# Later rows of a partition added to PSUM by VectorE in place of identity matmuls, with the pipeline drained at each tile

## Chip, cores, metric

One core of one Trainium2 chip. The metric is the device time of one execution in microseconds (us), the median of several runs. The kernel before takes 1262.9 us. Its runs agree within 0.1%.

## The reference

A running log-sum-exp along the second axis of a float32 array of shape (4, 4096, 4128). It equals the log of a running sum of exps:

```python
out[:, 0, :] = x[:, 0, :]
for t in range(1, S):
    mx = np.maximum(out[:, t - 1, :], x[:, t, :])
    out[:, t, :] = mx + np.log(np.exp(out[:, t - 1, :] - mx) + np.exp(x[:, t, :] - mx))
```

## The kernel before

A tile is 128 partitions by R rows by 4128 columns. R is 3 in 40 tiles and 2 in 4 tiles; the first tile and the last are two-row tiles. Partition p holds R consecutive rows. There are four tile buffers, so loads run three tiles ahead. A tile is worked on in four chunks of 1024 columns; the last chunk also has a tail of 32 columns. For each chunk ScalarE (ACT in the profile) takes the exp of all rows. TensorE (PE; its weight loads are PEld) then forms, in one of three PSUM buffers (`pt`, the memory that matmuls add into; `qt` is the same for the tail), the sum of everything up to the first row of each partition: triangular matmuls (`incl`, `excl`) over the rows, and a `pick` matmul for the carry. This group is called a head below.

The rows then come out one at a time, each in a "stage": ACT writes the Ln of the PSUM buffer to the tile, and then the next row's exps are added to the same buffer. In the kernel before, an identity matmul does that addition. After the last row VectorE (DVE) saves the last 32 partitions as the carry of the next tile, as a pair of fp16 values: a cast and a subtract.

```python
def keep(cr, pt):
    nc.vector.tensor_copy(cr[HI:HI + 32, :], pt[HI:HI + 32])
    nc.vector.tensor_tensor(out=cr[LO:LO + 32, :], in0=pt[HI:HI + 32],
                            in1=cr[HI:HI + 32, :], op=mybir.AluOpType.subtract)
# ... class Chunk
def stage(self, j):
    t, c, pt = self.t, self.c, self.pt
    nc.scalar.activation(t.xt[:, j, c * CH:(c + 1) * CH], pt, ACT.Ln)
    if j + 1 < t.r:
        for s in range(0, CH, MM):
            mm(pt[:, s:s + MM], ident, self.e(j + 1, s, s + MM), stop=j + 2 == t.r)
        if c == last and j == 0:
            nc.scalar.activation(t.xt[:, :, t0:D], self.qt, ACT.Ln)      # the tail Ln
            keep(carry_t, self.qt[:, t.r - 1, :])
    else:
        keep(carry[c], pt)
# ... the loop runs over the chunks of ALL tiles, three chunks in flight
for g in range(len(chunks) + R - 1):
    for d in range(R - 1, -1, -1):
        if 0 <= g - d < len(chunks) and d < chunks[g - d].t.r:
            k = chunks[g - d]
            k.stage(d)
            # ... after a tile's last stage: store it, load three tiles ahead
    if g + 2 < len(chunks):
        chunks[g + 2].exp()
    if g + 1 < len(chunks):
        chunks[g + 1].head()
```

The softmax here doesn't subtract the row's maximum and nothing guards it: scores larger than these inputs give would overflow.

## Time and profile before

| | before |
|---|---|
| time, median | 1262.9 us |
| queue's share of the 16 transfer engines | 99.4% |
| busy: ACT, PE, DVE | 947, 689, 451 us |
| one three-row tile: transfers, compute when not waiting | 29.2 us, 22.7 us |

The last row of the table is read from the exps of the last chunk. Their starts are 29.2 us apart on average in the steady state, and 22.7 us apart where two tiles run back to back.

The page of the kernel before follows. The line that begins with DMA is the mean busy share of the transfer engines in tenths, in 40 slices of the span (the time from the first to the last instruction). The two lines after the queue line are the chain that ended last, by engine and by instruction. The last two are groups: count, busy us, mean ns of one, idle time before them and its releaser.

```profile
span 1261.0 us, 6165 instructions
...
PE 688.7 (55%) x2268; PEld 237.0 (19%) x2268; DVE 451.4 (36%) x445; ACT 947.3 (75%) x733; POOL 2.2 (0%) x13
...
DMA  9999999999999999999999999999999999999998
...
q1 hardware_dynamic: 12672, 541.07, 99.4%
...
DMA 69%; ACT 21%; PE 5%; issue 2%; DVE 1%; SPq 0%; ACTq 0%
DMA xt<-in_x_dram 67%; ACT xt L128 11%; ACT xt L162 10%; PE pt L88 5%; DMA out_dram<-xt 2%; ACT xt L167 0%; SPq L116 0%; DVE carry L92 0%; DVE carry L93 0%; ACTq L231 0%; SPq L113 0%; ACTq L128 0%; PE qt L88 0%
...
L88 PE MATMUL pt<-xt,ident 128*128 128x512 f16 x672 | 251.3, 470 | 530.7 <-ACT xt L162 530.4
...
L93 DVE TENSOR_TENSOR carry<-pt,carry 32x1024 f16<-32x1024 f32 x176 | 215.9, 1227 | 6.1
```

The queue is full in every slice but the last, and loads are 67% of the chain: this kernel is held by its transfers. The skill's "DMA: Bandwidth & Descriptors", section "Where 436 GB/s comes from", gives 435 GB/s as the ceiling of the ports into SBUF. This trace moved 429 GB/s on average and 432 to 433 in a steady stretch, just under that figure, so it agrees.

From its waits view (engine, instruction, what it waited for, total us, times, longest):

```profile
ACT xt L128 <- DMA xt<-in_x_dram: 247.8, 42, 12.2
ACT xt L167 <- PE pt L88: 45.7, 44, 1.1
```

The first line is the slack: exps wait 248 us in total for loads, about 6 us per tile. The tail Ln (L167) reads only `qt`, yet in every tile it waits for a matmul on `pt`, the identity matmul issued just before it. (It writes the last 32 columns of `xt`; that matmul reads other columns of the same tile.)

### The profile page before, as it was taken

The page shows a single profiled execution, that of the slowest core. Times are in us where ns is not written, and L with a number is a line of the kernel's source. Part 1 is how long each engine was busy: PE and PEld are TensorE (multiplying, and loading weights), DVE is VectorE, ACT ScalarE, POOL GpSimd, SP SyncE. Part 2 cuts the span into 40 slices and gives each one's busy share as a digit, 9 for nine tenths or more (in the row PEclk, how much of TensorE's full clock was granted, in tenths as well). Part 3 has the DMA queues.
Part 4 walks back from the last instruction along what each step waited for, and adds up shares of the span by engine and source line. Part 5 has one row for each costly group of instructions (what it writes and reads, how often), then busy time and mean ns, then how long its engine had stood idle before and what let it go on. Part 6 is the DMA issues. An engine that isn't in the chain of part 4 may idle for free.

```text
span 1261.0 us, 6165 instructions
## 1 busy us (share of the span) xinstructions
PE 688.7 (55%) x2268; PEld 237.0 (19%) x2268; DVE 451.4 (36%) x445; ACT 947.3 (75%) x733; POOL 2.2 (0%) x13
## 2 busy tenths in 40 slices
PE   3665554555555555655346555555634755664552
PEld 1222111111121111211112211111211211221120
DVE  2443333333333333334424333333442433333344
ACT  5997777777777777778569777777966977777794
POOL 0000000000000000000000000000000000000000
PEclk9887777777677777777768777787777777778786
DMA  9999999999999999999999999999999999999998
GB/s 411 410 439 431 432 427 434 438 430 432 433 437 431 432 432 436 432 427 436 431 433 436 437 429 431 436 436 432 430 434 435 432 431 432 434 435 431 433 422 347
DMA packets 12702, 541.46 MB, mean 429 GB/s; under 512 B 1408, under 2 KB 1408, under 8 KB 1408
## 3 DMA queue, kind: packets, MB, share of 16 engines
q1 hardware_dynamic: 12672, 541.07, 99.4%
q8 instruction: 18, 0.29, 0.1%
q14 instruction: 12, 0.10, 0.0%
HBM read 270.53 MB, written 270.53 MB: 429 GB/s over the span
## 4 chain that ended last, share of the span: by engine, by line
DMA 69%; ACT 21%; PE 5%; issue 2%; DVE 1%; SPq 0%; ACTq 0%
DMA xt<-in_x_dram 67%; ACT xt L128 11%; ACT xt L162 10%; PE pt L88 5%; DMA out_dram<-xt 2%; ACT xt L167 0%; SPq L116 0%; DVE carry L92 0%; DVE carry L93 0%; ACTq L231 0%; SPq L113 0%; ACTq L128 0%; PE qt L88 0%
## 5 line engine op out<-in xcount | busy, mean ns | idle before, releaser
L128 ACT ACTIVATE xt<-xt 128x3072 f16<-128x3072 f32 (+3 forms) x176 | 478.5, 2719 | 247.9 <-DMA xt<-in_x_dram 247.8
L88 PE MATMUL pt<-xt,ident 128*128 128x512 f16 x672 | 251.3, 470 | 530.7 <-ACT xt L162 530.4
L162 ACT ACTIVATE xt<-pt 128x1024 f32<-128x1024 f32 x512 | 487.6, 1030 | 2.5 <-PE pt L88 0.7
L92 DVE CAST carry<-pt 32x1024 f16<-32x1024 f32 x176 | 216.4, 1230 | 761.0 <-ACT xt L162 760.7
L88 PE MATMUL pt<-xt,excl 128*128 128x512 f16 x672 | 247.0, 504 | 0.0
L93 DVE TENSOR_TENSOR carry<-pt,carry 32x1024 f16<-32x1024 f32 x176 | 215.9, 1227 | 6.1
L88 PEld LDWEIGHTS <-ident 128*128 128x128 f16 x672 | 70.1, 104 | 677.7 <-issue 654.0
L88 PE MATMUL pt<-xt,incl 128*128 128x512 f16 x352 | 152.0, 526 | 23.6 <-ACT xt L128 15.0
L88 PEld LDWEIGHTS <-excl 128*128 128x128 f16 x756 | 92.5, 124 | 141.0 <-issue 108.1
L88 PE MATMUL pt<-carry,pick 128*128 128x512 f16 x320 | 109.8, 429 | 0.0
L88 PEld LDWEIGHTS <-incl 128*128 128x128 f16 x480 | 45.2, 111 | 129.7 <-DVE carry L93 95.2
L88 PEld LDWEIGHTS <-pick 128*128 128x128 f16 x360 | 40.6, 113 | 57.0 <-issue 34.3
L167 ACT ACTIVATE xt<-qt 128x96 f32<-128x96 f32 (+1 forms) x44 | 10.9, 249 | 45.7 <-PE pt L88 45.7
L92 DVE CAST carry_t<-qt 32x32 f16<-32x32 f32 x44 | 8.7, 197 | 25.5 <-ACT xt L167 25.4
L88 PE MATMUL qt<-xt,incl 128*128 128x64 f16 (+2 forms) x128 | 12.3, 196 | 0.0
L88 PE MATMUL qt<-xt,excl 128*128 128x64 f16 (+1 forms) x84 | 10.6, 187 | 0.0
L93 DVE TENSOR_TENSOR carry_t<-qt,carry_t 32x32 f16<-32x32 f32 x44 | 8.5, 193 | 1.5
L88 PE MATMUL qt<-carry_t,pick 128*128 128x96 f16 (+1 forms) x40 | 8.2, 204 | 0.0
L83 DVE MEMSET carry<- 128x512 uint32 x4 | 1.9, 485 | 1.1 <-PEq L220 1.0
L70 ACT ACT_TABLE_LOAD x1 | 1.3, 1283 | 0.8 <-PEq L220 0.8
L35 POOL TENSOR_SCALAR_AFFINE_SELECT pick<-pick 128x128 f16<-128x128 f16 x2 | 0.6, 294 | 0.1
L25 POOL TENSOR_SCALAR_AFFINE_SELECT incl<-incl 128x128 f16<-128x128 f16 x1 | 0.3, 294 | 0.0
(11 smaller groups left out, 1.9 us busy)
## 6 DMA issues: line engine op xcount, KB each, us to landing
xt<-in_x_dram SPq DMA_DIRECT2D x40, 6192.0 KB, 42.2
out_dram<-xt SPq DMA_DIRECT2D x40, 6192.0 KB, 28.1
xt<-in_x_dram SPq DMA_DIRECT2D x4, 4128.0 KB, 37.3
out_dram<-xt SPq DMA_DIRECT2D x4, 4128.0 KB, 23.0
```

Source lines behind the costliest of these rows:

```text
L25: nc.gpsimd.affine_select(out=t, in_=t, pattern=[[1, P]], compare_op=mybir.AluOpType.is_ge, fill=0.0, base=base, channel_multiplier=-1,)
L35: nc.gpsimd.affine_select(out=t, in_=t, pattern=[[step, P]], compare_op=mybir.AluOpType.not_equal, fill=1.0, base=base, channel_multiplier=1,)
L70: nc.scalar.preload_act_table_set("natural_log_exp_and_others")
L83: nc.vector.memset(t, 0.0)
L88: nc.tensor.matmul(pt, lhsT=w, rhs=rhs, start=start, stop=stop, skip_group_check=True)
L92: nc.vector.tensor_copy(cr[HI:HI + 32, :], pt[HI:HI + 32])
L93: nc.vector.tensor_tensor(out=cr[LO:LO + 32, :], in0=pt[HI:HI + 32], in1=cr[HI:HI + 32, :], op=mybir.AluOpType.subtract,)
L128: nc.scalar.activation(self.t.half[:, :, 2 * c0:2 * c0 + w], self.t.xt[:, :, c0:c0 + w], ACT.Exp,)
L162: nc.scalar.activation(t.xt[:, j, c * CH:(c + 1) * CH], pt, ACT.Ln)
L167: nc.scalar.activation(t.xt[:, :, t0:D], self.qt, ACT.Ln)
```

## The change

The intent is to take the identity matmuls off TensorE, which needs a weight load for each, and to give the additions to VectorE, which is idle 64% of the time. The loop is rewritten tile by tile: each tile's stages all end before the next tile's first exp is issued. The diff, cut to its core:

```diff
-                for s in range(0, CH, MM):
-                    mm(pt[:, s:s + MM], ident, self.e(j + 1, s, s + MM), stop=j + 2 == t.r)
+                nc.vector.tensor_tensor(
+                    out=pt, in0=pt, in1=self.e(j + 1, 0, CH), op=mybir.AluOpType.add,
+                )
 ...
-    for g in range(len(chunks) + R - 1):
-        for d in range(R - 1, -1, -1):
-            if 0 <= g - d < len(chunks) and d < chunks[g - d].t.r:
-                k = chunks[g - d]
-                k.stage(d)
 ...
+    for n, s in enumerate(steps):
+        chunks = [Chunk(s, c) for c in range(n_main)]
+        chunks[0].exp()
+        chunks[1].exp()
+        chunks[0].head()
+        for g in range(n_main + s.r - 1):
+            for d in range(s.r - 1, -1, -1):
+                if 0 <= g - d < n_main:
+                    chunks[g - d].stage(d)
+            if g + 2 < n_main:
+                chunks[g + 2].exp()
+            if g + 1 < n_main:
+                chunks[g + 1].head()
+        s.store()
+        if n + ahead < len(steps):
+            steps[n + ahead].load()
```

The identity matrix and its construction go too. Bytes moved and work on ACT are unchanged.

More of the change, by code (lines that the diff above doesn't have):

```diff
@@ L29, in tri, with ones_at @@
         return t
-    def ones_where_zero(bases, step, name):
+    def ones_at(rows, name):
         t = pool.tile([P, P], FP16, name=name)
         nc.gpsimd.memset(t, 0.0)
-        for base in bases:
+        for row in rows:
             nc.gpsimd.affine_select(
-                out=t, in_=t, pattern=[[step, P]], compare_op=mybir.AluOpType.not_equal,
-                fill=1.0, base=base, channel_multiplier=1,
+                out=t, in_=t, pattern=[[0, P]], compare_op=mybir.AluOpType.not_equal,
+                fill=1.0, base=-row, channel_multiplier=1,
             )
@@ L43, in _constants @@
         tri(-1, "excl"),
-        ones_where_zero([0], -1, "ident"),
-        ones_where_zero([-(HI + 31), -(LO + 31)], 0, "pick"),
+        ones_at([HI + 31, LO + 31], "pick"),
     )
@@ L71 @@
     consts = ctx.enter_context(tc.tile_pool(name="consts", bufs=1))
-    incl, excl, ident, pick = _constants(nc, consts)
+    incl, excl, pick = _constants(nc, consts)
     bufs = 4
@@ L85, with mm @@
     ctx.enter_context(tc.manual_schedule())
-    def mm(pt, w, rhs, start=False, stop=False):
-        nc.tensor.matmul(pt, lhsT=w, rhs=rhs, start=start, stop=stop, skip_group_check=True)
+    def mm(pt, w, rhs, start=False):
+        nc.tensor.matmul(pt, lhsT=w, rhs=rhs, start=start, stop=False, skip_group_check=True)
     def keep(cr, pt):
@@ L182 @@
         assert row == S
-    chunks = [Chunk(s, c) for s in steps for c in range(n_main)]
     ahead = bufs - 1
@@ L187 @@
         s.load()
-    stored = 0
-    chunks[0].exp()
-    chunks[1].exp()
-    chunks[0].head()
-    for g in range(len(chunks) + R - 1):
-        for d in range(R - 1, -1, -1):
-            if 0 <= g - d < len(chunks) and d < chunks[g - d].t.r:
-                k = chunks[g - d]
-                k.stage(d)
-                if k.c == last and d + 1 == k.t.r:
-                    k.t.store()
-                    if stored + ahead < len(steps):
-                        steps[stored + ahead].load()
-                    stored += 1
-        if g + 2 < len(chunks):
-            chunks[g + 2].exp()
-        if g + 1 < len(chunks):
-            chunks[g + 1].head()
+    for n, s in enumerate(steps):
[14 more added lines that the diff above has]
+            steps[n + ahead].load()
 _INS = ['x']
```

## The prediction

> **What bounds it now.** The DMA queues. The profile's queue table gives the one data queue 99.4% of the span on 16 engines, 541 MB at 429 GB/s, and the slice view shows 9 tenths in every slice. The Trainium skill, "DMA: Bandwidth & Descriptors", section "Where 436 GB/s comes from", puts the port ceiling at 435 GB/s; the trace agrees. A tile of three rows per partition (R=3) moves 12.4 MB, about 29 us; two tiles take 58.5 us in the chain of waits. Compute fits inside: ACT is busy 947 us (75%), about 22 us per tile, DVE 451 us, and the waits view has ACT waiting 248 us for loads, mostly once every two tiles. Slack: about 6 us per tile.
>
> **What the change does.** It removes 672 identity matmuls (470 ns, 251 us of PE), off the critical path, and adds 336 VectorE adds over 128x1024. Their cost: the carry subtract has the same operands (fp32 PSUM, fp16 SBUF, 1024 columns) and took 1.227 us. The Trainium skill, "VectorE: DVE Perf Modes", errata section, gives (N+151)/0.96 for an fp32 tensor_tensor, 1224 ns here; agrees. At 1.25 us each: +420 us of DVE, to about 870 us. The next tile's exps and first matmuls no longer stand among this tile's last Lns.
>
> **Critical path.** No engine exceeds 29 us per tile in sum (ACT 22, DVE 20), but the chain does. One R=3 tile laid out by hand in program order (exp 2.76 us, next start 2.66 later; Ln 1.03, every 0.93; cold matmul 0.43, so 8 take 3.5; carry pair 2.5; hand-offs about 0.05):
> - exp0, exp1, then ACT waits about 1 us for the first chunk's matmuls; Ln, exp2, two Lns, exp3, Ln: 15.7 us.
> - From there VectorE leads: carry0, add, add, carry1, add, add (to 25.7 us). The tail Ln has a wait on VectorE in the new build, so it waits for the last of these adds and stands ahead of chunk 2's last Ln: carry2 starts at about 27.0, last add ends at 30.7.
> - The last Ln ends at 31.8; the next exp0 starts at about 31.7.
> R=2 tiles, likewise: 23 us. DMA needs 29 us per R=3 tile, so compute becomes the bound.
> Total: 27.7 (first exp, as before) + 40 x 31.7 + 4 x 23.0 + about 13 (last 4.1 MB store and end) = 1401 us, 11% slower.
>
> **Prediction:** 1400 us, 8 in 10 between 1365 and 1440. Chances: faster by over 2% 0.01, within 2% 0.03, slower by over 2% 0.96.
>
> **What would show each step.** Queue share falls to about 0.90 and GB/s to about 387; ACT's wait for loads falls to under 40 us. In its place ACT waits for VectorE adds (about 5 to 7 us per tile) and for first-chunk matmuls (about 1 us). Adds: 336, mean 1.2 to 1.25 us; DVE busy 850 to 880 us; ACT busy unchanged at about 947 us. The chain that ended last: DVE near half, ACT near half, DMA under 6%. Exp0 starts every 31 to 32 us in R=3 tiles.
>
> **What would make it wrong.** An add whose output is in PSUM has no record in this trace; if it costs 1.1 us, the period falls by about 0.8 us (1370), if 1.4, it grows by 0.8 (1435). A faster TensorE clock at the tile's start saves at most 1 us per tile (1360). If the tile period came under 29 us, DMA would bind again and the time would be the same as before, nearly 3 us below my layout. Late loads (stores holding the fourth buffer) would add time.

## The result and the profile after

The changed kernel takes 1382.3 us, against 1262.9 us for the kernel before: a ratio of 1.0945, with a 95% interval of 1.0926 to 1.0964. A ratio here is the mean time of one kernel's runs over that of the other's in the same rounds, so it is not quite the ratio of the medians that are quoted.

The page of the changed kernel, the same lines. The last but one is the new add; the identity group is gone.

```profile
span 1380.2 us, 5327 instructions
...
PE 482.2 (35%) x1596; PEld 182.3 (13%) x1596; DVE 853.4 (62%) x781; ACT 974.1 (71%) x733; POOL 1.8 (0%) x11
...
DMA  9999999999999999998999999999899999999847
...
q1 hardware_dynamic: 12672, 541.07, 93.2%
...
DVE 42%; ACT 42%; PE 10%; issue 4%; DMA 1%; ACTq 0%
ACT xt L126 25%; DVE pt L162 18%; ACT xt L160 16%; DVE carry L90 12%; DVE carry L91 12%; PE pt L86 10%; DMA xt<-in_x_dram 1%; ACT xt L166 1%; ACTq L227 0%; ACTq L166 0%; ACTq L160 0%
...
L162 DVE TENSOR_TENSOR pt<-pt,xt 128x1024 f32<-128x1024 f32 x336 | 402.0, 1229 | 316.5 <-ACT xt L160 312.4
...
L91 DVE TENSOR_TENSOR carry<-pt,carry 32x1024 f16<-32x1024 f32 x176 | 215.9, 1227 | 6.1
```

Transfers fell from 69% to 1% of the chain, and ACT and DVE share it in equal parts. No compute engine is busy more than 71% of the span. The busiest resource is still the queue, at 93%; run e4 shows that it no longer sets the time.

From its waits view:

```profile
ACT xt L160 <- DVE pt L162: 211.9, 88, 2.9
...
ACT xt L166 <- DVE pt L162: 117.5, 44, 3.0
ACT xt L160 <- PE pt L86: 32.3, 40, 0.9
...
ACT xt L126 <- DMA xt<-in_x_dram: 11.1, 1, 11.1
```

Exps (L126) wait once for a load, the first. Lns (L160) and the tail Ln (L166) wait for adds 329 us in total, 7.5 us per tile, and 32 us for the head of a tile's first chunk.

The second part of one three-row tile, on the timeline (start, duration, engine, line, operation, tiles, shapes, count merged, and idle time before with its releaser). L90 and L91 are a carry pair. Where ACT shows three Lns merged, they are of three different chunks.

```profile
650.55 2.85 ACT L160 ACTIVATE xt<-pt 128x1024 f32<-128x1024 f32 x3
651.61 1.23 DVE L90 CAST carry<-pt 32x1024 f16<-32x1024 f32 x1 [2.34 <-ACT xt L160]
652.87 1.23 DVE L91 TENSOR_TENSOR carry<-pt,carry 32x1024 f16<-32x1024 f32 x1
654.13 2.36 DVE L162 TENSOR_TENSOR pt<-pt,xt 128x1024 f32<-128x1024 f32 x2
...
655.40 3.14 ACT L160 ACTIVATE xt<-pt 128x1024 f32<-128x1024 f32 x3 [1.99 <-DVE pt L162]
...
656.52 1.23 DVE L90 CAST carry<-pt 32x1024 f16<-32x1024 f32 x1
...
657.79 1.23 DVE L91 TENSOR_TENSOR carry<-pt,carry 32x1024 f16<-32x1024 f32 x1
659.05 2.37 DVE L162 TENSOR_TENSOR pt<-pt,xt 128x1024 f32<-128x1024 f32 x2
...
661.50 0.25 ACT L166 ACTIVATE xt<-qt 128x96 f32<-128x96 f32 x1 [2.97 <-DVE pt L162]
661.65 1.93 ACT L160 ACTIVATE xt<-pt 128x1024 f32<-128x1024 f32 x2
...
662.70 1.23 DVE L90 CAST carry<-pt 32x1024 f16<-32x1024 f32 x1 [0.49 <-ACT xt L160]
663.97 1.23 DVE L91 TENSOR_TENSOR carry<-pt,carry 32x1024 f16<-32x1024 f32 x1
665.22 1.23 DVE L162 TENSOR_TENSOR pt<-pt,xt 128x1024 f32<-128x1024 f32 x1
666.49 1.02 ACT L160 ACTIVATE xt<-pt 128x1024 f32<-128x1024 f32 x1 [2.90 <-DVE pt L162]
667.41 3.84 ACT L126 ACTIVATE xt<-xt 128x2048 f16<-128x2048 f32 x2
```

From 651.61 to 666.45 VectorE has only two gaps of any size, 0.38 and 0.49 us, before and after the small tail carry (not shown) at 661.79. It works through carry, two adds, carry, two adds, the small tail carry, carry, add. ACT follows it: it waits 2 to 3 us at a time for one more buffer to be ready. The next tile's exp starts only behind the last Ln, at 667.41. In the first half of the tile it is the other way round: ACT is nearly always busy and VectorE has only three adds and the carry left over from the tile before. So neither engine is full over a tile, but one of the two is full at nearly all times.

### The profile page after: what moved, and what is told of

It reads as the page before. It is cut to its first block, busy times and chain, and to the rows that moved or that the text cites. A ratio compares the mean times of both kernels' runs of the same rounds, so it can differ in the third digit from the quotient of the medians.

```text
span 1380.2 us, 5327 instructions
## 1 busy us (share of the span) xinstructions
PE 482.2 (35%) x1596; PEld 182.3 (13%) x1596; DVE 853.4 (62%) x781; ACT 974.1 (71%) x733; POOL 1.8 (0%) x11
## 4 chain that ended last, share of the span: by engine, by line
DVE 42%; ACT 42%; PE 10%; issue 4%; DMA 1%; ACTq 0%
ACT xt L126 25%; DVE pt L162 18%; ACT xt L160 16%; DVE carry L90 12%; DVE carry L91 12%; PE pt L86 10%; DMA xt<-in_x_dram 1%; ACT xt L166 1%; ACTq L227 0%; ACTq L166 0%; ACTq L160 0%
## 5 line engine op out<-in xcount | busy, mean ns | idle before, releaser
L160 ACT ACTIVATE xt<-pt 128x1024 f32<-128x1024 f32 x512 | 505.0, 1023 | 263.4 <-DVE pt L162 211.9
L162 DVE TENSOR_TENSOR pt<-pt,xt 128x1024 f32<-128x1024 f32 x336 | 402.0, 1229 | 316.5 <-ACT xt L160 312.4
L126 ACT ACTIVATE xt<-xt 128x3072 f16<-128x3072 f32 (+3 forms) x176 | 475.5, 2701 | 12.5 <-DMA xt<-in_x_dram 11.1
L90 DVE CAST carry<-pt 32x1024 f16<-32x1024 f32 x176 | 216.4, 1230 | 175.4 <-ACT xt L160 174.1
L86 PE MATMUL pt<-xt,excl 128*128 128x512 f16 x672 | 259.2, 524 | 0.0
L91 DVE TENSOR_TENSOR carry<-pt,carry 32x1024 f16<-32x1024 f32 x176 | 215.9, 1227 | 6.1
L86 PEld LDWEIGHTS <-incl 128*128 128x128 f16 x480 | 53.3, 117 | 965.0 <-issue 926.1
L86 PE MATMUL pt<-carry,pick 128*128 128x512 f16 x320 | 128.1, 491 | 0.0
L86 PEld LDWEIGHTS <-excl 128*128 128x128 f16 x756 | 95.7, 128 | 146.7 <-issue 117.6
L166 ACT ACTIVATE xt<-qt 128x96 f32<-128x96 f32 (+1 forms) x44 | 10.9, 249 | 117.5 <-DVE pt L162 117.5
L86 PEld LDWEIGHTS <-pick 128*128 128x128 f16 x360 | 43.9, 122 | 64.8 <-issue 47.3
L90 DVE CAST carry_t<-qt 32x32 f16<-32x32 f32 x44 | 8.6, 196 | 16.8 <-ACT xt L166 16.8
L86 PE MATMUL qt<-xt,incl 128*128 128x64 f16 (+2 forms) x128 | 15.9, 233 | 0.0
L91 DVE TENSOR_TENSOR carry_t<-qt,carry_t 32x32 f16<-32x32 f32 x44 | 8.5, 193 | 1.5
```

The lines of the kernel that those rows point to most:

```text
L86: nc.tensor.matmul(pt, lhsT=w, rhs=rhs, start=start, stop=False, skip_group_check=True)
L126: nc.scalar.activation(self.t.half[:, :, 2 * c0:2 * c0 + w], self.t.xt[:, :, c0:c0 + w], ACT.Exp,)
L162: nc.vector.tensor_tensor(out=pt, in0=pt, in1=self.e(j + 1, 0, CH), op=mybir.AluOpType.add,)
```

## The experiments

The theory: a three-row tile's time is the longer of its transfers (29.2 us) and its compute period. The change lengthens the compute period in two ways, by adds on VectorE and by draining, and only the two together push it past 29.2 us. Rivals: the adds alone do it; the drain alone does it; transfers that come late set part of the new period. Each run was timed beside runs of its own of the kernel before, and differences within 2% count as "same".

All kernels were correct except e4 to e7, which leave most of the output unwritten. Their outputs are wrong, which doesn't matter for the times.

### e1: the adds alone

The identity matmuls in `stage` become the VectorE add as in the diff above; the loop over all chunks stays as before.

> The adds on VectorE, but the loop of the kernel before, so that the next tile's first exps and matmuls stand among this tile's last Lns. Theory (neither part alone takes a tile past the 29 us that its transfers take; only both together do): about 1263 us, 1255 to 1275, with the queue still above 98% of the span; a tile laid out by hand takes 25 to 26 us of compute. Rival (the adds alone put VectorE on the critical path): 1300 us or more, with ACT waiting for adds over 150 us and the queue below 96%.

Measured: 1276.6 us, ratio 1.0107 (1.0092 to 1.0123); queue 98.8%. This is just above the range given, and slower than before by 13.7 us, but far from the rival's 1300 us. One mark of the rival was met: ACT waited 152 us for adds, where it had over 150; its other two, time and queue share, were not. Where are the 13.7 us? Mostly at the two ends, where there is no queue of ready transfers to hide compute behind. The fourth store, which the loads behind it wait for, goes out at 121.6 us in place of 115.7, and the fifth at 151.0 in place of 144.9: about 6 us. In between the lag grows slowly, to 10.7 us at the last load: from 150 to 1190 us the queue's share is 1.00 in both kernels, but it moves 431 GB/s in place of 433, and the exps of the last chunk start 29.33 us apart on average in place of 29.19. The cause of this lag is not known. The last 3.6 us come at the end. In windows of 10 us (the columns are the busy us of PE, PEld, DVE, ACT and POOL, then the granted TensorE clock, the queue's share, which in so short a window can pass 1, and GB/s), the kernel before has

```profile
1230.00:1240.00 10.00, 6.73 (x22) 2.31 (x22) 7.75 (x8) 9.29 (x9) 0.00 (x0) 0.83 0.63 269
1240.00:1250.00 10.00, 1.90 (x12) 0.72 (x10) 6.48 (x7) 3.13 (x4) 0.00 (x0) 0.71 1.03 444
```

and the adds-only kernel has

```profile
1230.00:1240.00 10.00, 5.30 (x20) 2.02 (x20) 8.29 (x9) 6.77 (x7) 0.00 (x0) 0.77 0.84 362
1240.00:1250.00 10.00, 4.04 (x10) 1.26 (x11) 8.68 (x8) 9.53 (x9) 0.00 (x0) 0.57 0.39 168
```

Its queue is 61% idle from 1240 to 1250, while the last tile is still computed: its last Ln ends near 1263, against 1244 before. The period theory stands, but 1263 us was too simple: slower compute shows at the ends even when the transfers bind in between.

### e2: the drain alone

The loop of the changed kernel, with the identity matmuls kept.

> Identity matmuls as before, but the loop of the changed kernel, which finishes every tile before the next one's first exp. Theory: about 1263 us, 1255 to 1275, since a tile laid out by hand takes 25 to 27 us of compute, under the 29 us of its transfers. Rival (draining is what costs, the adds only replace matmuls): 1300 us or more, with exps starting 30 us or more apart from tile to tile.

Measured: 1263.4 us, ratio 1.0004 (0.9987 to 1.0021); queue 99.4%. The rival falls. Exps of the last chunk start 27.3 us apart where tiles run back to back, and about 29 us apart on average in the steady state.

### e3: the tail Ln moved off the chain

The changed kernel, with the tail moved behind the last chunk's last Ln:

```diff
-                if c == last and j == 0:
-                    nc.scalar.activation(t.xt[:, :, t0:D], self.qt, ACT.Ln)
-                    keep(carry_t, self.qt[:, t.r - 1, :])
             else:
+                if c == last:
+                    nc.scalar.activation(t.xt[:, :, t0:D], self.qt, ACT.Ln)
                 keep(carry[c], pt)
+                if c == last:
+                    keep(carry_t, self.qt[:, t.r - 1, :])
```

> The changed kernel with the tail Ln and tail carry moved behind the last chunk's last Ln, so that chunk 2's last Ln no longer stands behind a tail Ln that waits for an add. Theory (that wait is on the chain, about 1.25 us of a three-row tile): period of three-row tiles 30.4 us in place of 31.7, time about 1332 us, 1322 to 1345. Rival (the wait is beside the chain; VectorE has as much to do either way, so it is paid elsewhere): 1375 to 1385 us.

Measured: 1340.9 us, ratio to the kernel before 1.0618 (1.0602 to 1.0634), so 41.4 us less than the changed kernel. The period of three-row tiles is 30.62 us. VectorE on the timeline of this run:

```profile
639.37 2.36 DVE L162 TENSOR_TENSOR pt<-pt,xt 128x1024 f32<-128x1024 f32 x2
641.77 1.23 DVE L90 CAST carry<-pt 32x1024 f16<-32x1024 f32 x1
643.03 1.23 DVE L91 TENSOR_TENSOR carry<-pt,carry 32x1024 f16<-32x1024 f32 x1
644.29 1.23 DVE L162 TENSOR_TENSOR pt<-pt,xt 128x1024 f32<-128x1024 f32 x1
```

The two adds are now followed at once by the third carry, where the changed kernel had the tail's wait, the tail carry and a 0.49 us gap (1.28 us from the end of the adds to the cast). This gives 40 x 1.06 = 42 us, close to the 41.4 measured. I had expected 50; the tail Ln now takes its 0.13 us ahead of the next exp, and the two-row tiles gain nothing, as their next Ln waits for that same add. The rival, that the wait is paid elsewhere, falls. So a third of the 119 us lost comes from where one 0.25 us instruction (with the 0.4 us tail carry that follows it on VectorE) stands in the program.

### e4: the changed kernel with fewer bytes

```diff
-            nc.sync.dma_start(out=self.dram(out), in_=self.xt)
+            nc.sync.dma_start(out=self.dram(out)[:, :, 3072:D], in_=self.xt[:, :, 3072:D])
```

> The changed kernel, storing only the last 1056 columns of each tile (wrong output on purpose): transfers fall to about 63% of the bytes, compute is the same. Theory (compute alone sets the changed kernel's period): tile period still 31.6 to 31.7 us; time 1365 to 1383 us, the few us off being the shorter last store. Rival (loads or stores that land late, or exps slowed by transfers, set part of it): under 1345 us.

Measured: 1374.8 us. The period is 31.67 us with the bytes at 63%. Its page:

```profile
q1 hardware_dynamic: 23424, 339.74, 60.6%
...
DVE 42%; ACT 42%; PE 10%; issue 4%; DMA 1%; ACTq 0%
```

The queue's share went from 93% to 61%, and the chain stayed as it was. Of the 7.5 us gained (0.5%) the shorter last store makes 6.8: the span ends 5.1 us after the last Ln, in place of 11.9. Late transfers do not set any part of the period that these runs can resolve.

### e5, e6, e7: the compute periods of the other three, bared

The same short store in the kernel before, in adds-only and in drain-only.

> The kernel before, storing only the last 1056 columns of each tile (wrong output on purpose; about 63% of the bytes), to bare its compute period. Theory (before is held by its transfers alone; two tiles that ran back to back in its trace started 22.7 us apart): three-row tiles 22 to 23 us apart, time 960 to 1010 us. Rival (compute is nearly as long as the transfers): over 1150 us.

> The adds-only kernel with the same short store. Theory (its tiles ran back to back 25.3 us apart in its trace, so the adds cost about 2.6 us of compute per tile, hidden by transfers of 29 us): tiles 25 to 25.7 us apart, time 1085 to 1130 us. Rival (the 13.7 us that the adds-only kernel lost is spread over all tiles, so its tiles are near the transfers' time): over 1230 us.

> The drain-only kernel with the same short store. Theory (27.3 us between back-to-back tiles in its trace): tiles 27 to 27.6 us apart, time 1170 to 1215 us. With e5 and e6 and the changed kernel's 31.7 us this shows whether the two costs add: 22.7, +2.6 and +4.6 would make 29.9, so about 1.8 us would be left that only both together bring.

Measured: 1001.0, 1121.2 and 1183.9 us, all three within the ranges given. After the first load, exps wait for loads 2.1 us in all in e5, 1.1 in e6 and not at all in e7, so these are compute periods. Two exps of the last chunk in consecutive three-row tiles, first in the kernel before with the short store,

```profile
605.91 2.89 ACT L128 ACTIVATE xt<-xt 128x3168 f16<-128x3168 f32 x1
628.64 2.89 ACT L128 ACTIVATE xt<-xt 128x3168 f16<-128x3168 f32 x1
```

then in adds-only,

```profile
623.21 2.84 ACT L128 ACTIVATE xt<-xt 128x3168 f16<-128x3168 f32 x1
648.51 2.83 ACT L128 ACTIVATE xt<-xt 128x3168 f16<-128x3168 f32 x1
```

then in drain-only,

```profile
455.07 2.83 ACT L128 ACTIVATE xt<-xt 128x3168 f16<-128x3168 f32 x1
482.38 2.84 ACT L128 ACTIVATE xt<-xt 128x3168 f16<-128x3168 f32 x1
```

and in the changed kernel as it is:

```profile
457.77 2.85 ACT L126 ACTIVATE xt<-xt 128x3168 f16<-128x3168 f32 x1
489.46 2.84 ACT L126 ACTIVATE xt<-xt 128x3168 f16<-128x3168 f32 x1
```

The differences are 22.73, 25.30, 27.31 and 31.69 us. They make the table:

| | loop over all chunks | drained at each tile |
|---|---|---|
| identity matmuls: compute period, time with full stores | 22.7 us, 1262.9 us | 27.3 us, 1263.4 us |
| VectorE adds: compute period, time with full stores | 25.3 us, 1276.6 us | 31.7 us, 1382.3 us |

The adds cost 2.6 us of compute per tile, the drain 4.6 us, and 1.8 us more come only with both. (This 1.8 is a remainder and not one cost: the drained kernel with matmuls has PE for 43% of its chain in e7 and DVE for 1%, the changed kernel PE for 10% and DVE for 42%. By e3, 1.06 us of the changed kernel's period is the place of the tail Ln; what that place costs the other three was not tested.) Transfers take 29.2 us, which the plain sum of the two costs, 29.9 us, would already pass. Three of the four periods lie below that and their differences hide behind it, apart from the ends of the run and e1's slow lag. The fourth lies 2.5 us above.

One more rival can be settled from the traces: the granted TensorE clock is 0.66 in the changed kernel and 0.77 before. But e1 had 0.64 and took 1276.6 us, and in the changed kernel ACT waits for matmuls 44 us in total, about 1 us per tile, against 329 us for adds. A slower TensorE is at most a small part of the loss.

### e10: half of the adds

Drained loop; the second row is added by VectorE, the third by identity matmuls.

```diff
+                if j == 0:
+                    nc.vector.tensor_tensor(
+                        out=pt, in0=pt, in1=self.e(1, 0, CH), op=mybir.AluOpType.add,
+                    )
+                else:
                     for s in range(0, CH, MM):
                         mm(pt[:, s:s + MM], ident, self.e(j + 1, s, s + MM), stop=j + 2 == t.r)
```

> Drained loop, but only the second row is added by VectorE; the third row is added by identity matmuls as before. Theory (a chain of VectorE work after the first chunk's last Ln sets the drained period; half the adds take about 2.5 us of it away, and a hand layout gives 28 us, below the 29.2 us of the transfers): back-to-back tiles 27.5 to 29 us apart, time 1262 to 1285 us. Rival (any add on VectorE in a drained tile costs the whole loss, for example by the hand-off itself or the tail's wait): tiles 30.5 us apart or more, over 1320 us.

Measured: 1263.5 us, ratio 1.0004 (0.999 to 1.0018); queue 99.4%; most three-row tiles follow each other at 28.3 to 28.6 us. The tail Ln still waits for an add in every tile of this kernel,

```profile
ACT xt L172 <- DVE pt L165: 66.8, 44, 3.0
```

and the loss is nevertheless gone. So it is the amount of work in the chain that counts, not the presence of a hand-off, and half of the adds are free even in the drained loop.

### e8 and e9: an attempt to beat both

In the kernel before, the queue is not quite full at the very end (the 0.63 above). In e8 the last two tiles are stored in four pieces each, chunk by chunk:

```diff
+        def store(self):
+            a = self.c * CH
+            nc.sync.dma_start(out=self.t.dram(out)[:, :, a:a + self.w], in_=self.t.xt[:, :, a:a + self.w])
 ...
+                late = d + 1 == k.t.r and k.t in steps[-2:]
+                if late:
+                    k.store()
                 if k.c == last and d + 1 == k.t.r:
-                    k.t.store()
+                    if not late:
+                        k.t.store()
```

> The kernel before, with the stores of its last two tiles cut into four, one per chunk, issued as each chunk is done. Theory (in the steady state the queue is full, so only the ends can be gained; the queue idles about 4 us before the last-but-one store and about 2 to 4 us around the last): 1249 to 1257 us, 0.5 to 1.1% faster. Rival (smaller packets cost what the earlier start gains): 1260 to 1266 us.

Measured: 1271.2 us, ratio 1.0067 (1.0054 to 1.0081), so 0.7% slower (within the 2% that counts as "same", but clear of the noise), which neither side expected. The reason is on ACT's timeline:

```profile
1253.46 1.96 ACT L132 ACTIVATE xt<-xt 128x2112 f16<-128x2112 f32 x1 [18.20 <-DMA out_dram<-xt]
```

The last tile's last exp waited 18.2 us for a store of other columns of the same tile. In e9 the last tile's first piece holds chunks 0 and 1 and is issued after that exp (`store` now takes the first chunk of the piece):

```diff
-                if late:
-                    k.store()
+                if late and k.t is steps[-2]:
+                    k.store(k.c)
+                elif late and k.c:
+                    k.store(0 if k.c == 1 else k.c)
```

> The kernel before with its last two tiles stored in pieces, mended after e8: in e8 the last tile's chunk-3 exp waited 18.2 us for a piece of its own tile's store, so the last tile's first piece is now issued only after that exp (chunks 0 and 1 together, then 2, then 3). Theory (the queue's idle time at the end is what can be gained, and e8 lost to that wait alone): 1249 to 1258 us, 0.4 to 1.1% faster. Rival (smaller packets themselves cost as much): 1260 us or more.

Measured: 1264.1 us, ratio 1.0009 (0.9996 to 1.0023): the same, as the rival had it. The wait is gone, and the gap is filled: from 1230 to 1240 us the queue has a share of 0.99 in place of 0.63. But from 1250 to 1260 it moves 243 GB/s, against 370 in the kernel before. The gain was given back in the last 10 us. Whether smaller packets or an uneven spread of the last pieces over the 16 engines does this was not tested and stays open. No kernel here beats the kernel before.

## Why the prediction was right

- **What binds before.** Right: the queue at 99.4%. (The 12.4 MB per tile in the prediction were a slip of units: 2 x 6192 KB of 1024 bytes are 12.7 MB, which at 432 GB/s take 29.4 us.) e5 adds that compute alone takes 22.7 us per tile, where the text had about 22.
- **Cost of the add.** Right: 336 adds of 1229 ns, against 1.2 to 1.25 us given; DVE busy 853 us, against 850 to 880.
- **The chain in a tile.** Right in every link that the timeline shows. From the tile's first exp, at 635.73, VectorE takes the lead after 15.9 us (15.7 given), carry2 starts after 27.0 (27.0) and the last add ends after 30.7 (30.7). The wait for the first head was given as about 1 us, and a typical tile shows 0.86. The tail Ln's wait for an add was foreseen from the order of the build, and e3 shows that it is on the chain. The three-row period, from first exp to first exp, was given as 31.7 us; it is 31.68 in most tiles and 31.57 on average. Two-row tiles: 23.0 given, 23.2 in a middle one.
- **Loads in time.** Right, by e4 and by the single wait of exps for a load.
- **ACT's waits.** The wait for adds was given as 5 to 7 us per tile and is 7.5. ACT busy was to stay at 947 us and is 974. The Lns take no longer each (1023 ns, before 1030). More of them stand alone, though, and busy time merges overlaps: two neighbours take 1.94 us together, two lone ones 1.02 us each.
- **The 18 us between 1400 and 1382.** The term that was mis-sized is "27.7 (first exp, as before)". That was a misreading: the exp at 27.7 us in the trace before is the second tile's. ACT's timeline of the kernel before:

```profile
13.08 3.85 ACT L128 ACTIVATE xt<-xt 128x2048 f16<-128x2048 f32 x2 [11.00 <-DMA xt<-in_x_dram]
...
27.68 2.76 ACT L128 ACTIVATE xt<-xt 128x3072 f16<-128x3072 f32 x1 [2.06 <-DMA xt<-in_x_dram]
```

The two-row exp (2048 elements) is the first tile's, at 13.08; in the changed kernel it starts at 13.19. That takes 14.5 us off, and 40 periods that are 0.13 us shorter take 5 us more; the end of the run gives 1 us back. The sum is then 1401 - 14.5 - 5.2 + 1 = 1382.

What the prediction did not say is how the loss divides: that each part alone would cost little or nothing, and that the place of one 0.25 us instruction holds a third of it. Only the runs showed that.

## What to carry to other kernels

Engines whose busy times all fit under the transfers can still miss them when the work of one comes first in a tile and that of another last: lay out one period in program order before moving work to an idle engine. Where a kernel is held by transfers, a change of compute shows little until it uses up the slack (e1 lost 1.1%, e2 nothing), and the next small one then costs in full; a run with fewer bytes bares the slack. If a small instruction with a long wait stands in an engine's program, look at what stands behind it, and move it to where nobody needs what follows.

## What the Trainium skill lacked or had wrong

- "Perfetto Trace Analysis", "Identifying the Most-Contended Engine", names the engine with the highest occupancy as the bottleneck (for transfers, HBM utilization in place of occupancy). In the changed kernel the queue is the busiest resource (93%, 392 GB/s over the span), yet e4 cut its bytes by 37% and the time fell by 0.5%. ACT (71%) and VectorE (62%) alternate in one chain. The page's section on dependency chains is the one that applies, but the page gives no test that tells the two cases apart; a run with fewer bytes did.
- "VectorE: DVE Perf Modes", errata section: its (N+151)/0.96 for an fp32 `tensor_tensor` add, from which we estimate 1224 ns at N=1024, also fits an add with input and output in PSUM and a second input in fp16 (1229 ns). The page states the formula for fp32 alone, and for operands in PSUM only a speed tier.
- "DMA: Bandwidth & Descriptors", "Where 436 GB/s comes from", says that between HBM and SBUF the HBM side (about 358 GB/s) binds. Here one core, loading and storing at once, moved 429 GB/s over the whole span. ("Perfetto Trace Analysis", "Roofline", does let a core that is alone active on its pair's memory pass 358, up to about 435, so it is this one sentence that misleads.)
- No page that I read says that a build may put a wait on an instruction for columns it does not touch: the tail Ln, which reads `qt` and writes the last columns of `xt`, waits for an add on `pt` that reads other columns of `xt` (117.5 us in total), and an exp waits for a store of other columns (18.2 us in e8). In both cases the two share the tile `xt`, which may be the reason; that was not tested.
